# A weight sum by an accumulating transfer, and two more products with hi and lo side by side, in the gate and up stage of a decoder layer

## The chip, the cores and the metric

One core of one Trainium2 chip. The metric is the device time of one execution in microseconds (us). Five engines work side by side: TensorE (PE; its weight loads are listed as PEld), VectorE (DVE), ScalarE (ACT), GpSimd (POOL) and SyncE (SP, which here only issues transfers). Each engine runs its own instructions in the order of its queue and waits on semaphores for the others.

## The reference

One layer of a decoder trunk in float32, with 512 positions and a model width of 1024: a mixer (stick-breaking attention and a gated convolution), a memory cross-attention, a SwiGLU channel sublayer and a final norm. The change touches the first half of the channel sublayer:

```python
hf = rms_norm(x, norm_ffn[l])
gate, up = jnp.split(hf @ w_ffn_in[l], 2, axis=-1)     # w_ffn_in: 1024 x 5632
x = x + (jax.nn.silu(gate) * up) @ w_ffn_out[l]        # w_ffn_out: 2816 x 1024
```

## The kernel before

**Numbers in two parts.** TensorE multiplies in a reduced float32 form (`F32R`). Each operand is split into a hi part (a cast, on ScalarE) and a lo part (the rest, a subtraction on VectorE, `rest_of`, L1006), and a product is the sum of hi x hi, hi x lo and lo x hi.

**Seven products for eight.** The gate and up products of the 2816 hidden columns are made in 22 blocks of 128 columns (`NF = 22`, block number `m`). Each block is a 2 x 2 block product (halves of the contraction; gate and up; halves of the positions), done in Strassen's way (Winograd's form) with seven products, numbered 0 to 6, instead of eight. That needs sums of weights and sums of activations. The activation forms `x2f[k][i]` are made once by `forms_of`, which returns for each of the seven products a hi and a lo part; for those made by `beside`, a third entry is one 512-wide tile with hi and lo next to each other.

**A product.** `product(ps, m, i)` runs over four tiles of the contraction (`KP = 4`). Where hi and lo lie side by side, it is one 512-wide matmul with the hi weights (L909) and one 256-wide one with the lo weights (L917), the four of the latter at the end of the product; the result is then the sum of both halves of the PSUM bank. Otherwise it is three 256-wide matmuls per tile (L914). Products 5 are done side by side in the blocks of `WIDE`.

**Weights of a block.** `ffn_load(m)` fetches two tiles: `wg` (two of the four parts of the weight block) and `ws` (a third part twice, onto which a POOL transfer adds the other two parts, L862). `load_corner` (L868, on SP) fetches the fourth part into a tile `a` of its own. VectorE then makes two more sums: `sum_third` (L874, in place in `wg[:, 0]`) and `sum_last` (L878, `wg[:, 0] + wg[:, 1]` into the second half of the corner tile). The casts are `pair_cast(m, 0)` for products 0 and 1, `pair_cast(m, 1)` for 4 and 2, `pair_cast(m, 2)` for 5 and 6 (the corner tile), `third_cast(m)` for 3 (from `wg[:, 0]`). `ws`, `wg` and the other weight tiles share a few buffers, so a load waits until the old tile in its buffer has been read.

**Results of a block.** Products 0, 3, 4 and 5 add up in one bank `z`, and `reads` copies what each stage needs out of it (ScalarE, L946; L944 in `WIDE` after product 5). Product 1 is in `v`, products 2 and 6 in `y`. `joined_halves` (L936, L937) adds the two halves of a bank to such a copy; `second` is the one for product 2, written to `sb`. `evict` part 0 multiplies by the norm factors (L960), part 1 is the silu (L962), part 2 (L971 in `WIDE`, L974 twice, L978 for even blocks) makes the activations of the second half of the sublayer.

**Order.** The order of TensorE, ScalarE and VectorE is written out by hand. `uses` lists the products: in the steady part 3, 2, 4 of block m, 0, 1 of block m+1, 5, 6 of block m. After each product come its `reads` and then the entries of `todo` under its number, in the order in which `at` put them in; `made` puts a cast at one number and its lo part one number later (two with `late=2`). POOL's and SP's queues are not in this list.

Of the kernel before, what the change touches and what calls it, by code (L numbers as in the profile page):

```python
# [11 lines left out]
ALU = mybir.AluOpType  # L12
# [13 lines left out]
NF = HID // P  # L26
HS = S // 2
# [17 lines left out]
def hybrid_layer(ctx: ExitStack, tc: tile.TileContext, xT_d, memT_d, mem_d, cols_d, wv_d, win_d,  # L45
                 wbr_d, wmix_d, wmq_d, wmk_d, wmv_d, wmo_d, wfi_d, wfo_d, gfin_d, out):
    nc = tc.nc
# [16 lines left out]
    def nm(s):  # L64
        count[0] += 1
        return f"{s}{count[0]}"
# [4 lines left out]
    def tmp(s, cols=512):  # L71
        return tpool.tile([P, cols], F32, tag="t", name=nm(s), padded_shape=[P, 512])

    def f(ap):
        return ap.bitcast(F32)
# [160 lines left out]
    first = nc.scalar.dma_start(gcol, cols_d)  # L236
# [398 lines left out]
    for m in range(KD):  # L635
        sig = []
        for j in range(2):
            if (m, j) not in gates:
                gate(m, j)
            t = gates.pop((m, j))  # L640
# [20 lines left out]
    for m in range(KD):  # L661
# [9 lines left out]
        t = tmp("km", MEM)  # L671
# [27 lines left out]
    def forms_of(xe, xo):  # L699

        b11, b12, b21, b22 = xe[:, :HS], xe[:, HS:], xo[:, :HS], xo[:, HS:]
        c, d = f(unit("c1")), f(unit("c2"))
        n1, t3, n2, t4 = c[:, :HS], c[:, HS:], d[:, :HS], d[:, HS:]
        nc.vector.tensor_tensor(out=n1, in0=b11, in1=b12, op=ALU.subtract)
        nc.vector.tensor_tensor(out=t3, in0=b22, in1=b12, op=ALU.subtract)
        nc.vector.scalar_tensor_tensor(out=n2, in0=n1, scalar=-1.0, in1=b22, op0=ALU.mult,  # L708
                                       op1=ALU.subtract)
        nc.vector.scalar_tensor_tensor(out=t4, in0=n2, scalar=-1.0, in1=b21, op0=ALU.mult,  # L710
                                       op1=ALU.subtract)
        u = unit("xf")
        nc.scalar.copy(u[:, :HS], b11)
        nc.vector.tensor_tensor(out=u[:, HS:], in0=b11, in1=f(u[:, :HS]), op=ALU.subtract)
        a, b = slice(0, HS), slice(HS, S)

        def beside(src, s):
            both = unit(s)
            nc.scalar.copy(both[:, a], src)
            nc.vector.tensor_tensor(out=both[:, b], in0=src, in1=f(both[:, a]), op=ALU.subtract)  # L720
            return both[:, a], both[:, b], both

        first = beside(b21, "xo")
        second, fourth = beside(n1, "xc"), beside(t3, "xc")
        third, fifth = beside(n2, "xd"), beside(t4, "xd")
        last = beside(b22, "xo")
        return [(u[:, a], u[:, b]), first, second, third[:2], fourth[:2], fifth, last]

    def residual(w_dram, act, old, gain, pairs=False):

# [56 lines left out]
    for h in range(MH):  # L787
        q = q_next
        scs = []
        for t2 in range(2):  # L790
            ps = ztile("sc")
            scs.append(ps)
            for i in range(2):
                t = 2 * t2 + i
# [5 lines left out]
        for t2 in range(2):  # L800
# [6 lines left out]
                                           in1=r1s[:, 2 * t2:2 * t2 + 2], op0=ALU.mult,  # L807
# [3 lines left out]
            for i in range(2):  # L811
                t = 2 * t2 + i
# [5 lines left out]
            for i in range(2):  # L818
                nc.vector.tensor_scalar(out=pr[:, i * MEM:(i + 1) * MEM],
                                        in0=pr[:, i * MEM:(i + 1) * MEM],  # L820
# [22 lines left out]

    KP = KD // 2
    raws, corners = {}, {}

    def ffn_load(m):

# [15 lines left out]

    def load_corner(m):

        a22 = corners[m] = fpool.tile([P, 2, 512], F32, tag="w2", name=nm("a22"))
        i = nc.sync.dma_start(a22[:, 0, :], wfi_d[m][:, 3 * 512:])  # L868
        if m < 2:
            after(i, [loads[-6]])  # L870

    def sum_third(m, eng=nc.vector):
        wg, s13 = raws[m]
        eng.tensor_tensor(out=wg[:, 0, :], in0=s13[:, 1, :], in1=wg[:, 0, :], op=ALU.add)  # L874

    def sum_last(m, eng=nc.vector):
        wg = raws[m][0]
        eng.tensor_tensor(out=corners[m][:, 1, :], in0=wg[:, 0, :], in1=wg[:, 1, :], op=ALU.add)  # L878

    wforms = {}  # L880

    def pair_cast(m, which):

        raw = (*raws[m], corners[m])[which]
        hi = wpool.tile([P, 2, 512], F32R, tag="wh", name=nm("wf"))
        lo = wpool.tile([P, 2, 512], F32R, tag="wl", name=nm("wf"))
        nc.scalar.copy(hi, raw)
        for n, i in enumerate(((0, 1), (4, 2), (5, 6))[which]):
            wforms[m, i] = hi[:, n, :], lo[:, n, :]
        return raw, hi, lo  # L890
# [11 lines left out]
    def product(ps, m, i, ks=range(KP)):  # L902

        rests = []
        for k in ks:
            hi, lo = (w[:, k * P:(k + 1) * P] for w in wforms[m, i])
            xh, xl, *both = x2f[k][i]
            if both and (i != 5 or m in WIDE):
                nc.tensor.matmul(ps, hi, both[0], start=i < 3 and k == 0, stop=False,  # L909
                                 skip_group_check=True)  # L910
                rests.append((ps[:, :HS], lo, xh))
                continue
            for j, (a, b) in enumerate(((hi, xh), (hi, xl), (lo, xh))):
                nc.tensor.matmul(ps[:, :HS], a, b, start=i < 3 and k == 0 and j == 0,  # L914
                                 stop=k == KP - 1 and j == 2, skip_group_check=True)
        for operands in rests:
            nc.tensor.matmul(*operands, start=False,  # L917
                             stop=ks[-1] == KP - 1 and operands is rests[-1],
                             skip_group_check=True)

    WIDE = range(5, NF - 3)
    banks, silus = {}, []
    acts = {}

# [10 lines left out]
    def joined_halves(out_, bank, old):  # L935
        nc.vector.tensor_tensor(out=out_, in0=bank[:, :HS], in1=old, op=ALU.add)  # L936
        nc.vector.tensor_tensor(out=out_, in0=bank[:, HS:], in1=out_, op=ALU.add)  # L937

    def reads(m, i):

        b = banks[m]
        z, s, t = b["z"][:, :HS], b["s"], b["t"]
        if i == 5 and m in WIDE:
            nc.scalar.copy(s[:, :HS], b["z"][:, HS:])  # L944
        elif i in (0, 3, 4):
            nc.scalar.copy((s[:, :HS], None, None, s[:, HS:], t[:, :HS])[i], z)  # L946
        elif i == 1:
            joined_halves(b["g"][:, :HS], b["v"], s[:, :HS])
        elif i == 6:
            joined_halves(b["g"][:, HS:], b["y"], s[:, HS:])  # L950

    def second(m):
        b = banks[m]
        joined_halves(b["t"][:, HS:], b["y"], b["t"][:, :HS])

    def evict(m, part):
        b = banks[m]
        g = b["g"]
        if part == 0:
            nc.vector.tensor_tensor(out=g, in0=g, in1=r2b[0], op=ALU.mult)  # L960
        elif part == 1:
            silus.append(nc.scalar.activation(g, g, AF.Silu))  # L962
        else:
            j, odd = divmod(m, 2)
            if not odd:
                acts[j] = f(unit("a1")), f(unit("a2"))
            to = slice(odd * HS, (odd + 1) * HS)
            first = b["z"][:, :HS]
            if m in WIDE:
                first = b["s"][:, :HS]  # L970
                nc.vector.tensor_tensor(out=first, in0=b["z"][:, :HS], in1=first, op=ALU.add)  # L971
            for half, u in enumerate((first, b["t"][:, HS:])):
                sl = slice(half * HS, (half + 1) * HS)
                nc.vector.scalar_tensor_tensor(out=acts[j][half][:, to], in0=u, scalar=-1.0,  # L974
                                               in1=g[:, sl], op0=ALU.mult, op1=ALU.mult)
            if not odd:
                n1 = acts[j][1][:, :HS]
                nc.vector.tensor_tensor(out=n1, in0=acts[j][0][:, :HS], in1=n1, op=ALU.subtract)  # L978
# [5 lines left out]
    m = NF - 1  # L984
# [134 lines left out]
    def at(n, *some):  # L1119
        todo.setdefault(n, []).extend(some)  # L1120

    def made(n, cast, *args, late=1):

        parts = []
        at(n, lambda: parts.append(cast(*args)))
        at(n + late, lambda: rest_of(*parts[0]))
# [14 lines left out]
    for m in range(1, NF - 1):  # L1141
        p = {i: uses.index((m, i)) for i in range(2, 7)}
        q = {i: uses.index((m + 1, i)) for i in range(2)}
        if m > 1:
            at(p[3], lambda m=m: sum_third(m + 1))
            at(p[3], lambda m=m: evict(m - 1, 0))
            at(p[2], lambda m=m: evict(m - 1, 1))
            at(q[0], lambda m=m: evict(m - 1, 2))
            made(p[3], pair_cast, m, 2)
            made(p[2], third_cast, m + 1)  # L1150
        else:
            made(p[4], third_cast, m + 1)
        at(p[4], lambda m=m: second(m))
        if m + 2 < NF:
            at(p[4], lambda m=m: load_corner(m + 2))
        made(q[0], pair_cast, m + 1, 1, late=2)
        at(q[1] if m < NF - 2 else p[4], lambda m=m: sum_last(m + 1))
        if m + 2 < NF:
            made(p[5], pair_cast, m + 2, 0)
    at(uses.index((0, 4)), lambda: second(0))  # L1160
# [33 lines left out]
    with tc.manual_schedule(engines={mybir.EngineType.PE, mybir.EngineType.Activation,  # L1194
# [69 lines left out]
        last = NJ - 2, NJ - 1  # L1264
# [17 lines left out]
        u = [plus("u", res[3][s2], s0[s2]) for s2 in range(2)]  # L1282
# [252 lines left out]
```

## Time and profile before

| | |
|---|---|
| median of 3 runs | 839.92 us (839.05 to 839.99) |
| the profiled execution | 838.75 us, its span 837.0 us |
| busy, share of the span | PE 828.8 us (99%), VectorE 684.6 (82%), ScalarE 463.9 (55%), POOL 161.2 (19%) |
| granted TensorE clock | 0.998 |
| traffic | 143.69 MB, mean 172 GB/s |

The span counts from the first to the last instruction; a row of a timeline gives the start and the duration in us, the engine, the line, the operation with `out<-in`, the shape and, in brackets, how long the engine had been idle before it and what released it. A release time of a wait is inferred from semaphores. Lines L909 to L917 and the others above are those of the code.

### The profile page before, as it was taken

What the parts mean: (1) busy time and instruction counts of PE and PEld (TensorE: products, weight loads), DVE (VectorE), ACT (ScalarE), POOL (GpSimd) and SP (SyncE); (2) the same over time, 40 slices, a digit from 0 to 9 for tenths busy, and PEclk for the clock granted to TensorE, in tenths of its full rate; (3) what the DMA queues carried; (4) which work ended last, traced back from release to release, by engine and by line L of the source; (5) the groups of instructions that cost most, each with busy time, mean ns of one, the idle gap of its engine ahead of it and who ended that gap; (6) DMA issues with size and microseconds to landing.
All of it is one profiled execution on the core that took longest, in us unless ns stands there. A gap on an engine that the chain in (4) does not pass through costs nothing.

```text
span 837.0 us, 11962 instructions
## 1 busy us (share of the span) xinstructions
PE 828.8 (99%) x4374; PEld 714.1 (85%) x4374; DVE 684.6 (82%) x1086; ACT 463.9 (55%) x796; POOL 161.2 (19%) x168
## 2 busy tenths in 40 slices
PE   9999999999999999999999999999999999999996
PEld 7888888888888888888888789999999999888885
DVE  7879899996756576587555698999999999999886
ACT  7567868674332355434444566645555555576654
POOL 0011131110566630173000031111111110000401
PEclk9999999999999999999999999999999999999999
DMA  8552435235687865566431326677767673465552
GB/s 303 155 166 101 122 111 103 74 115 174 228 312 276 304 249 188 182 233 249 148 82 51 101 51 161 167 184 200 197 180 197 176 184 95 170 213 197 180 183 101
DMA packets 51357, 143.69 MB, mean 172 GB/s; under 512 B 5761, under 2 KB 7041, under 8 KB 48482
## 3 DMA queue, kind: packets, MB, share of 16 engines
q1 hardware_dynamic: 41650, 107.89, 38.2%
q0 software_dynamic: 9360, 34.75, 15.8%
q8 instruction: 34, 0.56, 0.3%
q10 hardware_dynamic: 288, 0.28, 0.1%
q14 instruction: 25, 0.20, 0.1%
HBM read 125.20 MB, written 13.64 MB: 166 GB/s over the span
## 4 chain that ended last, share of the span: by engine, by line
PE 99%; DVE 0%; ACT 0%; DVEq 0%; issue 0%
PE z L914 13%; PE p L1228 12%; PE pr L161 8%; PE pr L162 8%; PE pr L163 8%; PE y L909 5%; PE r L162 3%; PE r L163 3%; PE r L161 3%; PE v L288 3%; PE y L917 2%; PE v L909 2%; PE km L666 2%; PE mq L163 2%; PE mq L161 2%; PE mq L162 2%
## 5 line engine op out<-in xcount | busy, mean ns | idle before, releaser
L156 ACT CAST wh<-wr 128x1024 fp32r<-128x1024 f32 x84 | 88.0, 1051 | 144.2 <-issue 80.0
L157 DVE TENSOR_TENSOR wl<-wr,wh 128x1024 fp32r<-128x1024 f32 x84 | 111.0, 1321 | 32.0 <-ACT wh L156 31.9
L161 PE MATMUL pr<-xgh,wh 128*128 128x512 f32 x288 | 112.8, 392 | 0.0
L162 PE MATMUL pr<-xgl,wh 128*128 128x512 f32 x288 | 112.4, 390 | 0.0
L163 PE MATMUL pr<-xgh,wl 128*128 128x512 f32 x288 | 112.3, 390 | 0.0
L611 POOL TENSOR_TENSOR pre<-pre 128x512 f32<-128x512 f32 x44 | 70.9, 1616 | 31.5 <-DMA pre<-in_w_ffn_out_dram 29.2
L862 POOL DMA_DIRECT2D ws<-in_w_ffn_in_dram x22 | 26.6, 1209 | 248.5 <-DVE c L708 54.0
L163 PEld LDWEIGHTS pr<-xgh,wl 128*128 128x128 f32 x288 | 54.1, 188 | 11.5
L161 PEld LDWEIGHTS pr<-xgh,wh 128*128 128x128 f32 x288 | 54.1, 188 | 10.6
L162 PEld LDWEIGHTS pr<-xgl,wh 128*128 128x128 f32 x288 | 54.1, 188 | 10.5
L914 PE MATMUL z<-xd,wf 128*128 128x256 f32 x360 | 47.5, 282 | 0.0
L946 ACT COPY sa<-z 128x256 f32<-128x256 f32 x44 | 16.4, 373 | 51.9 <-PE z L914 51.9
L914 PEld LDWEIGHTS z<-xd,wf 128*128 128x128 f32 x360 | 45.0, 190 | 0.1
L1006 DVE TENSOR_TENSOR wf<-wg,wf 128x1024 fp32r<-128x1024 f32 (+1 forms) x44 | 43.1, 978 | 1.5
L1006 DVE TENSOR_TENSOR wl<-wr,wh 128x1024 fp32r<-128x1024 f32 x33 | 41.0, 1242 | 1.8 <-ACT wh L1073 1.8
L1073 ACT CAST wh<-wr 128x1024 fp32r<-128x1024 f32 x33 | 34.5, 1050 | 5.3 <-ACT f01h L1002 2.6
L914 PE MATMUL z<-xf,wf 128*128 128x256 f32 x264 | 35.4, 283 | 0.0
L914 PE MATMUL z<-xc,wf 128*128 128x256 f32 x264 | 35.1, 283 | 0.0
L914 PEld LDWEIGHTS z<-xf,wf 128*128 128x128 f32 x264 | 33.4, 192 | 0.1
L914 PEld LDWEIGHTS z<-xc,wf 128*128 128x128 f32 x264 | 33.0, 190 | 0.0
L368 DVE TENSOR_TENSOR g<-pr,r0b 128x512 f32<-128x512 f32 x16 | 11.0, 687 | 23.5 <-PE pr L163 23.5
L417 POOL TENSOR_SCALAR_AFFINE_SELECT e<-e 128x128 f32<-128x128 f32 (+1 forms) x24 | 10.7, 447 | 86.6 <-DVE e L470 86.6
(356 smaller groups left out, 2239.9 us busy)
## 6 DMA issues: line engine op xcount, KB each, us to landing
wr<-in_w_in_dram SPq DMA_DIRECT2D x36, 512.0 KB, 3.4
pre<-in_w_ffn_out_dram POOLq DMA_DIRECT2D x11, 1024.0 KB, 8.0
sums<-pre POOLq DMA_DIRECT2D x11, 1024.0 KB, 5.0
ws<-in_w_ffn_in_dram SPq DMA_DIRECT2D x22, 512.0 KB, 4.8
wg<-in_w_ffn_in_dram SPq DMA_DIRECT2D x22, 512.0 KB, 4.7
ws<-in_w_ffn_in_dram POOLq DMA_DIRECT2D x22, 512.0 KB, 5.7
wr<-sums SPq DMA_DIRECT2D x22, 512.0 KB, 4.0
wr<-in_w_ffn_out_dram SPq DMA_DIRECT2D x16, 512.0 KB, 3.7
```

The costliest lines, as they stand in the source:

```text
L156: after(nc.scalar.copy(h2, raw), lead[-1:])
L157: lows.append(nc.vector.tensor_tensor(out=l2, in0=raw, in1=f(h2), op=ALU.subtract))
L161: nc.tensor.matmul(ps, a[0], b[0], start=start, stop=False, **kw)
L162: nc.tensor.matmul(ps, a[0], b[1], start=False, stop=False, **kw)
L163: nc.tensor.matmul(ps, a[1], b[0], start=False, stop=stop, **kw)
L611: nc.gpsimd.tensor_tensor(out=t[:, a, :], in0=t[:, a, :], in1=t[:, b, :], op=ALU.add)
L862: nc.gpsimd.dma_start(s13, a[:, 0:4:3, :], accum_op=ALU.add)
L909: nc.tensor.matmul(ps, hi, both[0], start=i < 3 and k == 0, stop=False, skip_group_check=True)
L914: nc.tensor.matmul(ps[:, :HS], a, b, start=i < 3 and k == 0 and j == 0, stop=k == KP - 1 and j == 2, skip_group_check=True)
L1006: nc.vector.tensor_tensor(out=lo, in0=src, in1=f(hi), op=ALU.subtract)
L1073: nc.scalar.copy(hi, raw)
L1228: nc.tensor.matmul(res[i][s2], a[:, ts], b, start=j == 0 and n == 0, stop=n == 2 and j == (BEHIND - 1 if (i, s2) == (5, 1) else NJ - 1))
```

## The change

For blocks 3 to 20 (`OWN`) the corner has no tile of its own any more. The sum of `sum_last` is made by an accumulating transfer on POOL, which adds `wg[:, 0]` onto `wg[:, 1]` in place, right after `sum_third`. After that, and after `third_cast` has been read out, `load_corner` fetches the fourth part into `wg[:, 0]`, so that `wg` itself becomes the corner tile. The load's place in the list is product 5 of the iteration before; `pair_cast(m, 2)` stands at product 4 instead of product 3, and its lo part at product 0 of the next block instead of product 2.

`WIDE` grows from blocks 5 to 18 to blocks 3 to 19, and in it product 4 is side by side too, since `forms_of` now hands out the joint tile for it. Then `reads` copies the whole bank `z` after product 4 (512 columns instead of 256), and `second` becomes `folded`: one 512-wide addition of the bank of product 2 to that copy, and one that adds the two halves. The copy after product 5 goes to `sb` instead of `sa`.

```diff
         second, fourth = beside(n1, "xc"), beside(t3, "xc")
         third, fifth = beside(n2, "xd"), beside(t4, "xd")
         last = beside(b22, "xo")
-        return [(u[:, a], u[:, b]), first, second, third[:2], fourth[:2], fifth, last]
+        return [(u[:, a], u[:, b]), first, second, third[:2], fourth, fifth, last]
 
     def residual(w_dram, act, old, gain, pairs=False):
 
 
     KP = KD // 2
     raws, corners = {}, {}
+    OWN = range(3, NF - 1)
 
     def ffn_load(m):
 
 
     def load_corner(m):
 
+        if m in OWN:
+            nc.sync.dma_start(raws[m][0][:, 0, :], wfi_d[m][:, 3 * 512:])
+            return
         a22 = corners[m] = fpool.tile([P, 2, 512], F32, tag="w2", name=nm("a22"))
         i = nc.sync.dma_start(a22[:, 0, :], wfi_d[m][:, 3 * 512:])
         if m < 2:
 
     def sum_last(m, eng=nc.vector):
         wg = raws[m][0]
+        if m in OWN:
+            nc.gpsimd.dma_start(wg[:, 1, :], wg[:, 0, :], accum_op=ALU.add)
+            return
         eng.tensor_tensor(out=corners[m][:, 1, :], in0=wg[:, 0, :], in1=wg[:, 1, :], op=ALU.add)
 
     wforms = {}
 
     def pair_cast(m, which):
 
-        raw = (*raws[m], corners[m])[which]
+        raw = (*raws[m], raws[m][0] if m in OWN else corners[m])[which]
         hi = wpool.tile([P, 2, 512], F32R, tag="wh", name=nm("wf"))
         lo = wpool.tile([P, 2, 512], F32R, tag="wl", name=nm("wf"))
         nc.scalar.copy(hi, raw)
         for k in ks:
             hi, lo = (w[:, k * P:(k + 1) * P] for w in wforms[m, i])
             xh, xl, *both = x2f[k][i]
-            if both and (i != 5 or m in WIDE):
+            if both and (i not in (4, 5) or m in WIDE):
                 nc.tensor.matmul(ps, hi, both[0], start=i < 3 and k == 0, stop=False,
                                  skip_group_check=True)
                 rests.append((ps[:, :HS], lo, xh))
                              stop=ks[-1] == KP - 1 and operands is rests[-1],
                              skip_group_check=True)
 
-    WIDE = range(5, NF - 3)
+    WIDE = range(3, NF - 2)
     banks, silus = {}, []
     acts = {}
 
 
         b = banks[m]
         z, s, t = b["z"][:, :HS], b["s"], b["t"]
-        if i == 5 and m in WIDE:
-            nc.scalar.copy(s[:, :HS], b["z"][:, HS:])
+        if m in WIDE and i == 4:
+            nc.scalar.copy(t, b["z"])
+        elif m in WIDE and i == 5:
+            nc.scalar.copy(t[:, :HS], b["z"][:, HS:])
         elif i in (0, 3, 4):
             nc.scalar.copy((s[:, :HS], None, None, s[:, HS:], t[:, :HS])[i], z)
         elif i == 1:
         elif i == 6:
             joined_halves(b["g"][:, HS:], b["y"], s[:, HS:])
 
+    def folded(out_, bank, old):
+        nc.vector.tensor_tensor(out=old, in0=bank, in1=old, op=ALU.add)
+        nc.vector.tensor_tensor(out=out_, in0=old[:, :HS], in1=old[:, HS:], op=ALU.add)
+
     def second(m):
         b = banks[m]
+        if m in WIDE:
+            folded(b["t"][:, HS:], b["y"], b["t"])
+            return
         joined_halves(b["t"][:, HS:], b["y"], b["t"][:, :HS])
 
     def evict(m, part):
             to = slice(odd * HS, (odd + 1) * HS)
             first = b["z"][:, :HS]
             if m in WIDE:
-                first = b["s"][:, :HS]
+                first = b["t"][:, :HS]
                 nc.vector.tensor_tensor(out=first, in0=b["z"][:, :HS], in1=first, op=ALU.add)
             for half, u in enumerate((first, b["t"][:, HS:])):
                 sl = slice(half * HS, (half + 1) * HS)
         q = {i: uses.index((m + 1, i)) for i in range(2)}
         if m > 1:
             at(p[3], lambda m=m: sum_third(m + 1))
+            if m + 1 in OWN:
+                at(p[3], lambda m=m: sum_last(m + 1))
+                at(p[5], lambda m=m: load_corner(m + 1))
             at(p[3], lambda m=m: evict(m - 1, 0))
             at(p[2], lambda m=m: evict(m - 1, 1))
             at(q[0], lambda m=m: evict(m - 1, 2))
-            made(p[3], pair_cast, m, 2)
+            made(p[4] if m in OWN else p[3], pair_cast, m, 2)
             made(p[2], third_cast, m + 1)
         else:
             made(p[4], third_cast, m + 1)
         at(p[4], lambda m=m: second(m))
-        if m + 2 < NF:
+        if m + 2 < NF and m + 2 not in OWN:
             at(p[4], lambda m=m: load_corner(m + 2))
         made(q[0], pair_cast, m + 1, 1, late=2)
-        at(q[1] if m < NF - 2 else p[4], lambda m=m: sum_last(m + 1))
+        if m + 1 not in OWN:
+            at(q[1] if m < NF - 2 else p[4], lambda m=m: sum_last(m + 1))
         if m + 2 < NF:
             made(p[5], pair_cast, m + 2, 0)
     at(uses.index((0, 4)), lambda: second(0))
```

## The prediction

> **What bounds the kernel now.** I read the chain of waits first, then the windows of the gate and up stage by block, then the timelines of three engines over one block. TensorE is the chain:
>
> ```profile
> PE 99%; DVE 0%; ACT 0%; DVEq 0%; issue 0%
> ```
>
> Nothing waits for TensorE to be fed. The windows below are one block each (the columns are the stretch, its length, busy time of PE, PEld, DVE, ACT and POOL, the granted clock, DMA share, GB/s):
>
> ```profile
> 551.32:561.26 9.94, 9.94 (x74) 9.42 (x73) 9.54 (x18) 5.00 (x8) 1.20 (x1) 1.00 0.74 189
> 581.09:591.00 9.91, 9.91 (x69) 9.20 (x69) 9.66 (x17) 5.38 (x9) 1.06 (x2) 1.00 0.68 184
> ```
>
> The first is a block whose fifth product is in twelve matmuls, the second one whose fifth product is already side by side. The granted clock is 1.00. VectorE is busy for 9.66 of 9.91 us: it keeps up, with little to spare, so its order of work decides whether TensorE stays fed. I call "product i of block m" what the code calls (m, i). TensorE's order is 3, 2, 4 of block m, 0, 1 of block m+1, 5, 6 of block m. This is iteration m = 7 on TensorE, from product 3 (575.22) to product 6 (583.73); columns are start, duration:
>
> ```profile
> 575.22 1.59 PE L914 MATMUL z<-xd,wf 128*128 128x256 f32 x12
> ...
> 578.05 1.59 PE L914 MATMUL z<-xc,wf 128*128 128x256 f32 x12
> 579.49 1.60 PE L914 MATMUL z<-xf,wf 128*128 128x256 f32 x12
> 580.92 1.09 PE L909 MATMUL v<-xo,wf 128*128 128x512 f32 x4
> ...
> 582.33 1.09 PE L909 MATMUL z<-xd,wf 128*128 128x512 f32 x4
> 583.25 0.64 PE L917 MATMUL z<-xd,wf 128*128 128x256 f32 x4
> 583.73 1.09 PE L909 MATMUL y<-xo,wf 128*128 128x512 f32 x4
> ```
>
> VectorE in the same time:
>
> ```profile
> 575.42 0.42 DVE L936 TENSOR_TENSOR fg<-y,sa 128x256 f32<-128x256 f32 x1
> ...
> 577.47 0.69 DVE L874 TENSOR_TENSOR wg<-ws,wg 128x512 f32<-128x512 f32 x1
> 578.08 0.68 DVE L960 TENSOR_TENSOR fg<-fg,r0b 128x512 f32<-128x512 f32 x1
> 578.68 1.22 DVE L1006 TENSOR_TENSOR wf<-a,wf 128x1024 fp32r<-128x1024 f32 x1
> 579.97 0.69 DVE L1006 TENSOR_TENSOR wf<-wg,wf 128x512 fp32r<-128x512 f32 x1
> 580.58 0.42 DVE L936 TENSOR_TENSOR sb<-y,sb 128x256 f32<-128x256 f32 x1
> 581.03 0.42 DVE L937 TENSOR_TENSOR sb<-y,sb 128x256 f32<-128x256 f32 x1
> 581.37 0.41 DVE L971 TENSOR_TENSOR sa<-z,sa 128x256 f32<-128x256 f32 x1
> 581.82 0.42 DVE L974 SCALAR_TENSOR_TENSOR a<-sa,fg 128x256 f32<-128x256 f32 x1
> 582.16 0.42 DVE L974 SCALAR_TENSOR_TENSOR a<-sb,fg 128x256 f32<-128x256 f32 x1
> 582.62 0.42 DVE L978 TENSOR_TENSOR a<-a,a 128x256 f32<-128x256 f32 x1
> 582.96 0.41 DVE L936 TENSOR_TENSOR fg<-v,sa 128x256 f32<-128x256 f32 x1
> ...
> 583.75 0.68 DVE L878 TENSOR_TENSOR a<-wg 128x512 f32<-128x512 f32 x1
> 584.35 1.22 DVE L1006 TENSOR_TENSOR wf<-ws,wf 128x1024 fp32r<-128x1024 f32 x1
> ```
>
> The row at 578.68 is what matters: the lo half of the corner pair, the weights of products 5 and 6. It ends at 579.90, over 3 us before product 5 reads it (L917, 583.25). It also sits in a gap: the next instruction, at 579.97, has to wait for ScalarE's cast of the third weight, which waits in turn for L960:
>
> ```profile
> 576.85 0.37 ACT L946 COPY sa<-z 128x256 f32<-128x256 f32 x1 [1.46 <-PE z L914]
> 577.12 1.06 ACT L887 CAST wf<-a 128x1024 fp32r<-128x1024 f32 x1
> 578.79 0.63 ACT L962 ACTIVATE fg<-fg 128x512 f32<-128x512 f32 x1 [0.62 <-DVE fg L960]
> 579.33 0.61 ACT L895 CAST wf<-wg 128x512 fp32r<-128x512 f32 x1
> 579.84 0.36 ACT L946 COPY sb<-z 128x256 f32<-128x256 f32 x1
> ```
>
> That cast ends at 579.94, and L1006 starts at 579.97.
>
> **The change, part by part.** *Fewer matmuls.* A product in twelve takes 579.49 - 578.05 = 1.44 us, one side by side 583.73 - 582.33 = 1.40; the two windows differ by 0.03 us for one product, which I take. Product 4 changes in 17 blocks (3 to 19) and product 5 in three more (3, 4, 19): 20 x 0.03 = 0.6 us less, on the path.
>
> *The weight sum leaves VectorE.* L878 goes in 18 blocks (3 to 20), 584.35 - 583.75 = 0.60 us each. VectorE does not end last, so this gives nothing by itself.
>
> *The second combination on whole banks.* L936 and L937 at 580.58 occupied 581.37 - 580.58 = 0.79 us. Now there is one 128x512 add, 0.69 us (as L874; all 512-wide adds here lie near) and some 0.03 to the instruction that needs it, then a 256-wide one, after which the next starts 0.34 later: 1.06 us, so 0.27 more in 17 blocks. ScalarE's copy before it goes from 0.36 us to 0.58, from this row (median of a 512-wide copy out of PSUM):
>
> ```profile
> L1273 ACT COPY s<-p x2: 578/584/589, 773.7 to 774.2; 128x512 f32<-128x512 f32 x2
> ```
>
> It starts at 579.84 and ends at 580.42, before VectorE gets there at 580.58, so it costs nothing; were VectorE there earlier, it would be the limit.
>
> *The corner pair is cast later.* This is the step that costs. In blocks 3 to 20 the cast goes from behind product 3 to behind product 4, and its lo half from VectorE's place at 578.68 to the list of the next product, behind the entries already there: the four of `evict(m - 1, 2)` (L971, L974 twice, L978). The place given up is worth nothing: 579.97 stays, since the cast of the third weight sets it. VectorE idles about 1.2 us there, then has everything else ahead of the lo half. For block 7: 580.58 + 1.06 = 581.64 (L971); L971 to L978 and what follows took 582.96 - 581.37 = 1.59, so the lo half starts at 583.23 and ends at 584.45. ScalarE's hi half runs from 580.4 to 581.5 and is in time for product 5 at 582.33. The wide form reads lo only in its fifth matmul, L917, 583.25 less 0.03 for the shorter product 4 = 583.22. How fast TensorE follows VectorE shows in one place of the trace:
>
> ```profile
> 463.61 0.69 DVE L181 TENSOR_TENSOR oml<-om,omh 128x512 fp32r<-128x512 f32 x1 [1.54 <-ACT omh L179]
> ...
> 464.36 0.19 PEld L162 LDWEIGHTS r<-oml,wh 128*128 128x128 f32 x1 [0.24 <-DVE oml L181]
> ```
>
> The weight load follows 0.06 us after the end (464.30), and I add 0.11 for the matmul that has nothing to overlap it with: 0.17 in all, an estimate. Stall: 584.45 + 0.17 - 583.22 = 1.40 us. Where m is even, L978 is absent: 0.46 less, 0.94. In block 3 L971 is absent (block 2 is not side by side): 0.95. Block 20 keeps the narrow product 5, which needs lo at its third matmul, 0.24 after 582.33, and keeps the last weight sum in front (0.60); with no L978 and the old 0.79 the lo half ends at 584.32, so the stall is 1.92.
>
> Sum: 8 odd blocks (5 to 19) x 1.40 + 8 even ones (4 to 18) x 0.94 + 0.95 + 1.92 = 21.6; less 0.6 gives +21.0 us. It does not heal itself: the next iteration hangs on the end of product 6, which moves with the stall. VectorE behind the late lo half has L936/L937 (0.79) and L1006 (1.22) to do, until 586.5; product 6 also ends at about 586.5 (584.62 + 0.48 for L917 + 1.40), and the next L936 starts 0.20 after that, as at 575.42: it starts each block on time, and loses the same again.
>
> *The transfers.* The accumulating transfer waits for L874 (end 578.16). The one it resembles, L862 on POOL with 512 KB, lands so long after its issue (us):
>
> ```profile
> DMA to landing us min/median/max: 5.4/5.7/8.3
> ```
>
> The corner load, L868 on SP with 256 KB, moves behind it, since it overwrites what the sum read; it lands after
>
> ```profile
> DMA to landing us min/median/max: 2.4/3.0/6.4
> ```
>
> Together that is 8.7 us at the medians, 14.7 at the maxima. The cast needs the corner one period later, at 580.42 + 11.1 = 591.5, that is 13.3 us after 578.16, and may be 1.4 late before it delays the lo half. Behind the waiting instructions stand, on POOL, the accumulate of L862 for three blocks ahead and, on SP, the loads of `ws` and `wg`. `wg` now comes free only with the late lo half (584.45) instead of with L878:
>
> ```profile
> wg<-in_w_ffn_in_dram SPq DMA_DIRECT2D x22, 512.0 KB, 4.7
> ```
>
> It is there 5 us later, and the first cast of it comes about a period after that. So I take zero for the transfers. The bounds are zero and, where the corner load also queues on SP behind that load of `wg` and both take long, about 1 us per block. By the Trainium skill, "DMA: Bandwidth & Descriptors", section "Anatomy of one DMA", a POOL transfer takes about 2.0 us plus its bytes at 436 GB/s, 2.6 us here as an estimate; the sum would be the same 21.0, and this case's own accumulates (5.4 at least) are slower than that. On POOL it is 18 more issues of about 1.2 us (the one in the first window's POOL column), on an engine busy for some 1 us of ten.
>
> Ends of the unknown: VectorE at 580.28 instead of 580.58 (ScalarE's copy 0.20 behind product 4's end, as at 576.85 behind product 3's) takes 17 x 0.3 = 5 us off, and no restart cost 2 more: +14. The transfers add up to 18: +39. I take +21, from the rows of the block itself.
>
> **The rivals.**
>
> *The cover holds.* If the lo half comes out ahead of `evict(m - 1, 2)` on VectorE, it starts at 581.64 and ends at 582.86, before 583.05, when it is wanted: no stall, 0.6 us gained, 839.3. Point of decision: the lo half ends 0.94 us (even) or 1.40 (odd) earlier than worked out. For it: ScalarE and VectorE have less in sum than before. Against: VectorE's rows above run in exactly the written order. 11 in 100.
>
> *The transfers come late too.* If accumulate and corner load together exceed some 14.8 us, the cast waits and the pair is later still: at 1 us a block in 18 blocks, 861 + 18 = 879. For it: DMA share is already 0.68 to 0.74, and these tiles are held a period longer. Against: the medians. 7 in 100.
>
> *The clock.* If gaps of about 1 us made the throttle halve the clock for the rest of each block, 9.9 us a block would come on top: 861 + 17 x 9.9 = 1029. The windows show 1.00 but have no gaps. The Trainium skill, "TensorE: Matmul & The Clock Gate", section "Why this matters for your kernels", puts the limit at gaps of about 3 us; by that rule nothing happens here, and no row here shows a gap of that length. 2 in 100.
>
> **How the numbers follow.** The profiled execution took 838.75 us (span 837.0); the median is 839.92. 838.75 + 21.0 = 859.8, against the median 860.9; I say 861. My forecast has 80 in 100. Its bounds give 854 (+14) at the low end, and part of the transfers' cost (0.5 us a block) 870 at the high end; I open the low end to 852 for rounding in the stalls. Outside lie the cover case, the clock and most of the late transfers. What a measurement can tell from no change is 0.2%, 1.7 us: slower 0.89 (80 + 7 + 2); the cover case's 0.6 us is "same", 0.09, with 0.02 left for faster.
>
> **What would show it.** Right: L917 weight loads of z wait on L1006, once a block, about 1.4 and 0.9 us in turn; blocks of about 11.3 and 10.8 us; VectorE idle about 1.2 us before the 512-wide L1006, waiting for L895; the lo half of the corner right behind L974 or L978. Rival transfers: ScalarE's cast of the corner waits on a DMA. Cover: blocks of 9.88 us. I would be wrong if the list order on VectorE were not as read, or if product 5 needed lo later than its fifth matmul.

## The result and the profile after

The changed kernel takes 860.24 us (median of 5 runs, 860.0 to 860.63) against 839.64 (5 runs): 1.0247 times as long, 95% interval 1.0232 to 1.0262. The profiled execution's span is 858.3 us against 837.0, 21.3 more. The prediction said 861, +21.0.

The chain of waits on the page of after is no longer TensorE alone:

```profile
PE 78%; DVE 16%; ACT 3%; issue 2%; DVEq 0%
```

The waits of the gate and up stage (engine, line, what it waited for: us in total, times, longest). L924 was L917 before, L1022 was L1006, L902 was L895, L894 was L887:

```profile
PEld z L924 <- DVE wf L1022: 22.3, 17, 1.5
DVE wf L1022 <- ACT wf L902: 21.8, 18, 1.2
...
ACT wf L894 <- DMA wg<-in_w_ffn_in_dram: 0.2, 1, 0.2
```

In 17 blocks the lo weights of product 5 are late; in block 20, whose product 5 is narrow, they are late too, by L921. In 18 blocks VectorE idles 1.2 us for the cast of the third weight. ScalarE waited for a transfer once, for 0.2 us. Two blocks, an odd and an even one, as windows (columns as in the prediction):

```profile
564.23:575.49 11.26, 10.15 (x66) 8.93 (x64) 9.54 (x17) 5.49 (x10) 2.11 (x2) 1.00 0.84 201
575.49:586.29 10.80, 10.15 (x65) 8.92 (x64) 9.12 (x16) 5.49 (x10) 2.11 (x2) 1.00 0.80 196
```

They alternate so through the stage, but for the first (11.08 us) and the last. VectorE is busy for less of it than before (9.12 to 9.54 of some 11 us, 9.66 of 9.91 then): it has less to do, but it waits, and the lo half comes late in its order. Block 7 on TensorE, the block of the prediction's rows:

```profile
586.76 1.09 PE L916 MATMUL z<-xd,wf 128*128 128x512 f32 x4
588.96 0.74 PE L924 MATMUL z<-xd,wf 128*128 128x256 f32 x4 [1.11 <-DVE wf L1022]
589.54 1.09 PE L916 MATMUL y<-xo,wf 128*128 128x512 f32 x4
```

Product 5 takes 589.54 - 586.76 = 2.78 us, 1.38 more than 1.40. VectorE in the same block:

```profile
582.54 0.69 DVE L976 TENSOR_TENSOR fg<-fg,r0b 128x512 f32<-128x512 f32 x1
584.43 0.69 DVE L1022 TENSOR_TENSOR wf<-wg,wf 128x512 fp32r<-128x512 f32 x1 [1.21 <-ACT wf L902]
585.04 0.68 DVE L962 TENSOR_TENSOR sb<-y,sb 128x512 f32<-128x512 f32 x1
585.76 0.43 DVE L963 TENSOR_TENSOR sb<-sb 128x256 f32<-128x256 f32 x1
586.10 0.42 DVE L987 TENSOR_TENSOR sb<-z,sb 128x256 f32<-128x256 f32 x1
586.55 0.76 DVE L990 SCALAR_TENSOR_TENSOR a<-sb,fg 128x256 f32<-128x256 f32 x2
587.35 0.42 DVE L994 TENSOR_TENSOR a<-a,a 128x256 f32<-128x256 f32 x1
587.69 1.22 DVE L1022 TENSOR_TENSOR wf<-wg,wf 128x1024 fp32r<-128x1024 f32 x1
588.83 0.42 DVE L943 TENSOR_TENSOR fg<-v,sa 128x256 f32<-128x256 f32 x1
```

The row at 587.69 is the lo half of the corner pair. Before, it stood directly behind the multiplication by the norm factors (L976, there L960) and filled the gap that is now the 1.21 us in brackets. Now it stands behind L962 to L994 and ends at 588.91; the weight load of L924 follows at 588.96.

### The profile page after: what moved, and what is told of

It reads as the page before. It is cut to its first block, busy times and chain, and to the rows that moved or that the text cites. A ratio compares the mean times of both kernels' runs of the same rounds, so it can differ in the third digit from the quotient of the medians.

```text
span 858.3 us, 11822 instructions
## 1 busy us (share of the span) xinstructions
PE 833.4 (97%) x4294; PEld 708.8 (83%) x4294; DVE 682.9 (80%) x1071; ACT 467.3 (54%) x799; POOL 174.3 (20%) x186
## 4 chain that ended last, share of the span: by engine, by line
PE 78%; DVE 16%; ACT 3%; issue 2%; DVEq 0%
PE p L1248 12%; PE pr L161 8%; PE pr L162 8%; PE pr L163 8%; DVE wf L1022 7%; PE r L162 3%; PE r L161 3%; PE r L163 3%; PE v L288 3%; PE y L916 2%; PE km L666 2%; PE mq L163 2%; PE mq L161 2%; PE mq L162 2%; PE br L163 2%
## 5 line engine op out<-in xcount | busy, mean ns | idle before, releaser
L1022 DVE TENSOR_TENSOR wf<-wg,wf 128x1024 fp32r<-128x1024 f32 (+1 forms) x62 | 65.0, 1048 | 21.9 <-ACT wf L902 21.8
L863 POOL DMA_DIRECT2D ws<-in_w_ffn_in_dram x22 | 26.7, 1213 | 139.0 <-DVE c L707 52.9
L921 PE MATMUL z<-xd,wf 128*128 128x256 f32 x324 | 43.1, 283 | 1.6 <-DVE wf L1022 1.6
L894 ACT CAST wf<-wg 128x1024 fp32r<-128x1024 f32 x40 | 42.1, 1052 | 2.0 <-PE r L162 1.8
L1022 DVE TENSOR_TENSOR wl<-wr,wh 128x1024 fp32r<-128x1024 f32 x33 | 40.2, 1219 | 3.0 <-ACT wh L1089 2.8
L921 PEld LDWEIGHTS z<-xd,wf 128*128 128x128 f32 x324 | 40.6, 191 | 1.9 <-DVE wf L1022 1.9
L883 POOL DMA_DIRECT2D wg<-wg x18 | 16.6, 925 | 120.4 <-DVE wg L878 82.8
L921 PE MATMUL z<-xf,wf 128*128 128x256 f32 x264 | 35.4, 283 | 0.0
L921 PEld LDWEIGHTS z<-xf,wf 128*128 128x128 f32 x264 | 33.4, 192 | 0.1
L978 ACT ACTIVATE fg<-fg 128x512 f32<-128x512 f32 x22 | 13.9, 632 | 35.6 <-DVE fg L976 35.6
L953 ACT COPY sb<-z 128x256 f32<-128x256 f32 x17 | 6.3, 373 | 41.2 <-PE z L924 23.4
```

The costliest lines, as they stand in the source:

```text
L863: nc.gpsimd.dma_start(s13, a[:, 0:4:3, :], accum_op=ALU.add)
L1022: nc.vector.tensor_tensor(out=lo, in0=src, in1=f(hi), op=ALU.subtract)
```

## The experiments

Four runs pull the change's parts apart, four more isolate the late cast and seek a place where the sum costs nothing, and two settle what those left open. They stand here by topic. Each is compared with the kernel before on the same chip.

**The lo half ahead of evict part 2.** (`e1_lo_first`)

```diff
+            made(p[4] if m in OWN else p[3], pair_cast, m, 2)
             at(q[0], lambda m=m: evict(m - 1, 2))
-            made(p[4] if m in OWN else p[3], pair_cast, m, 2)
```

> The changed kernel with one move: on VectorE the lo half of the corner pair comes ahead of the entries of evict part 2 (m - 1) instead of behind them; hi cast, weight sum and products 4 and 5 stay. Theory A (the lo half is late only because of what stands ahead of it): it ends at 582.86 in the frame of block 7 of the prediction, in time, so the stall goes and the time is 839 to 840 us. Theory B (VectorE's cycle: L943/L944 0.80, lo of products 0 and 1 1.25, L878 0.61, L976 to the third weight's lo 1.89 because ScalarE's silu and cast lie between, that lo 0.61, L962/L963 1.06, corner lo 1.14, evict part 2 1.36 on average, L943/L944 0.79, lo of 4 and 2 1.14: 10.65 us a block, whatever the order, as long as the 1.2 us gap in front of the third weight's lo is empty; TensorE needs only 9.88): 17 x (10.65 - 9.88) and some 0.8 for block 20, less 0.6, is +13; 852 to 854 us, with the stalls now anywhere in the block.

852.86 us (852.53 to 852.98), ratio 1.0162 (1.0145 to 1.0179): theory B. The blocks, from product 1 to product 1:

```profile
583.45 1.09 PE L916 MATMUL v<-xo,wf 128*128 128x512 f32 x4
593.86 1.09 PE L916 MATMUL v<-xo,wf 128*128 128x512 f32 x4
604.71 1.09 PE L916 MATMUL v<-xo,wf 128*128 128x512 f32 x4
```

The two blocks take 10.41 and 10.85 us, 10.63 on average against the 10.65 of VectorE's cycle. The instructions in the cycle are shorter in sum than a block of TensorE; it is the gap that makes it longer:

```profile
594.11 0.69 DVE L1022 TENSOR_TENSOR wf<-wg,wf 128x512 fp32r<-128x512 f32 x1 [1.21 <-ACT wf L902]
```

VectorE multiplies (L976), ScalarE makes the silu and then casts the third weight, VectorE takes that cast: a round trip which VectorE used to fill with the lo half. With the order repaired but the gap still empty, two thirds of the loss stay.

**The cast back at its place.** (`e2_cast_back`)

```diff
-            made(p[4] if m in OWN else p[3], pair_cast, m, 2)
+            made(p[3], pair_cast, m, 2)
```

> The changed kernel with the cast of the corner pair back behind product 3 and its lo half back at product 2, where it fills VectorE's gap; weight sum by transfer, corner load into wg and products 4 and 5 side by side stay. Theory (the late cast alone made it slower): the stall at L924 goes; VectorE's cycle is 9.5 us. 839.5 us if sum and corner load land in time. They have 8.8 us from the end of L878 to the cast, 1.4 more before it hurts; in the changed kernel they took about 8.6 (3.7 and 4.1 us at the medians, with the waits between), so in some blocks the cast may wait for a transfer: up to 846. Rival (the transfers or the wider products cost the time themselves): still 855 to 861.

851.91 us (847.32 to 853.18), ratio 1.014 (1.0111 to 1.0169): a miss. The stall of product 5 at L924 is gone and many blocks take 9.88 to 9.89 us, but others take up to 11.8, and the times scatter (the profile is of the run of 847.32):

```profile
ACT wf L894 <- DMA wg<-in_w_ffn_in_dram: 41.4, 16, 4.2
```

I had the landing of the corner load too short. It took 2.8 to 7.3 us, 5.9 at the median, where 4.1 had been seen. It now follows 0.7 to 2.4 us behind the load of a `wg` tile on SP, where it went ahead of that load before; I take this to be the reason, but no run isolates it. So neither the theory's number nor the rival as put (products or transfers cost that much in the changed kernel) holds: the old place of the cast asks more of the transfers than the changed kernel did.

**The transfer and the late cast without the wider products.** (`e3_own_only`: `product`, `reads`, `second`, `evict`, `forms_of` and `WIDE` as before)

> The kernel before with the weight sum by transfer, the corner load into wg and the late cast in blocks 3 to 20 alone; product 4 stays in twelve matmuls, product 5 side by side in blocks 5 to 18 as before. Theory (order of VectorE's work): second is 0.27 us shorter, so the lo half ends 0.27 earlier and is wanted where it was: stalls of 1.10 (odd) and 0.64 (even) in the side by side blocks, 0.9 to 1.8 in blocks 3, 4, 19 and 20, whose narrow product 5 wants lo at its third matmul; sum 17, so 856 to 857 us. Rival (the wider products make it slow): about 840.

862.96 us (862.34 to 863.91), ratio 1.0283 (1.0267 to 1.0298). The stalls in the regular part are those expected: blocks of 10.99 and 10.54 us, that is 9.91 + 1.08 and + 0.63. Two blocks took 13.59 and 14.21 us, some 6.3 us more than their neighbours; without them it would be 856.7. In these ScalarE waits for the corner:

```profile
580.28 1.04 ACT L894 CAST wf<-wg 128x1024 fp32r<-128x1024 f32 x1 [3.67 <-DMA wg<-in_w_ffn_in_dram]
```

and on POOL the sum (L883) stood behind the accumulate of `ws` (L863), before which POOL had been idle for 12.02 us:

```profile
570.34 1.20 POOL L863 DMA_DIRECT2D ws<-in_w_ffn_in_dram  x1 [12.02 <-DVE wf L1017]
571.05 1.43 POOL L883 DMA_DIRECT2D wg<-wg  x1
```

The profile puts that wait down to VectorE. The accumulate also waits for the plain load of the same `ws` tile, issued on SP at 564.52, and I take that load to be what came last; it is inferred, not shown. Part of the 6.3 us is the clock: behind the two waits of TensorE in these blocks (1.54 and 2.44 us) the granted clock was 0.50 for some 3 us.

**The wider products alone.** (`e4_wide_only`)

```diff
-    OWN = range(3, NF - 1)
+    OWN = range(0)
```

> The kernel before with products 4 and 5 side by side in blocks 3 to 19 alone; the weight sum stays on VectorE and the corner in a tile of its own, cast behind product 3. Theory: 0.6 us less on TensorE, but VectorE's cycle grows from 9.84 to 10.11 us where TensorE needs 9.88; that lag of 0.23 us a block reaches 3.9 us over 17 blocks, of which some 2.2 us of lead on the other lo halves swallow most: about 1.7 us of stall in the last blocks, 840 to 841.5 us. Rival (VectorE keeps up): 839.1. If it is slower than 845, the wider products, not the late cast, made the change slow.

842.6 us (842.28 to 842.72), ratio 1.0039 (1.0024 to 1.0054). The mechanism holds: six blocks take 9.87 to 9.89 us, the ones behind them 10.08 to 10.16, VectorE's cycle with the sum still on it. The lead I gave it was too long (six blocks, not nine), hence 1.1 us past the range. VectorE (the third busy time of the row) in one of the later blocks, busy for 9.86 of 10.10 us:

```profile
644.00:654.10 10.10, 10.10 (x64) 8.81 (x64) 9.86 (x17) 5.27 (x10) 1.32 (x2) 1.00 0.66 174
```

So the wider products cost 3 us by themselves, as 0.27 us a block more on VectorE outweighs 0.03 less on TensorE; they need the sum off VectorE.

**The late cast alone.** (`e7_late_alone`, from the kernel before)

```diff
-            made(p[3], pair_cast, m, 2)
+            made(p[4] if m > 2 else p[3], pair_cast, m, 2)
...
-            at(p[4], lambda m=m: load_corner(m + 2))
+            at(p[5] if m > 2 else p[4], lambda m=m: load_corner(m + 2))
```

> The kernel before with the pair cast alone moved behind product 4 in blocks 3 to 20 (its lo half to product 0 of the next block), the corner's next load behind it; sum on VectorE, no accumulating transfer, products as before. Theory: VectorE's cycle is 0.80 + 1.25 + 0.61 + 1.89 + 0.61 + 0.79 + 1.36 + 1.14 + 0.79 + 0.60 + 1.14 = 10.98 us a block, more than the 11.01 and 10.54 (10.78) that the lo half's lateness gives: 17 x 1.07 + 1.5 for block 20 = +20, 857 to 860. Rival (the late cast costs only together with the transfers or the wider products): 839 to 845.

860.74 us (859.73 to 861.64), ratio 1.0254 (1.0239 to 1.0269), with no accumulating sum and no wider product in it. Blocks of 10.74 and 11.19 us, 10.97 on average against 10.98. The first took 13.65. In it TensorE stood still for 1.91 us and was then granted half its clock (the third number from the end of the second row) for some 3 us:

```profile
545.74 2.40 PE L914 MATMUL z<-xd,wf 128*128 128x256 f32 x10 [1.91 <-DVE wf L1006]
546.20:549.20 3.00, 3.00 (x13) 2.73 (x12) 2.01 (x3) 0.00 (x0) 0.00 (x0) 0.50 0.65 200
```

The matmuls behind that wait, up to the lo matmuls of product 6, took 2.19 + 1.56 us, against 1.30 + 0.93 for the same ones a block later: 1.5 us, more than the 0.7 us by which the time lies past the range. The late cast, with the later corner load that goes with it, is enough to lose all that the changed kernel loses. Its limit here is VectorE's cycle, which still has the sum on it; in the changed kernel it is the lateness of the lo half (11.03 us a block).

**A tile of its own for the corner.** (`e5_own_tile`; the cast is back behind product 3 and the load of the fourth part at its old place)

```diff
         i = nc.sync.dma_start(a22[:, 0, :], wfi_d[m][:, 3 * 512:])
+        if m in OWN:
+            nc.sync.dma_start(a22[:, 1, :], wfi_d[m][:, 512:2 * 512])
...
-            nc.gpsimd.dma_start(wg[:, 1, :], wg[:, 0, :], accum_op=ALU.add)
+            nc.gpsimd.dma_start(corners[m][:, 1, :], wg[:, 0, :], accum_op=ALU.add)
```

> The changed kernel with the corner back in a tile of its own: two loads (the fourth part and the second part of the weight block) as early as before the change, the third weight added onto the second half by the accumulating transfer, cast behind product 3 and lo half at product 2 as before the change; products 4 and 5 side by side in 3 to 19. Theory (a cycle of VectorE of 9.5 us, with the gap in front of the third weight's lo filled, and a sum that now lands some 4 us before it is wanted): no stall, 0.6 us less than before: 838.6. Rival (accumulating transfers disturb the other transfers or VectorE): above 840, with casts waiting on DMA.

850.98 us (849.04 to 853.28), ratio 1.0139 (1.0118 to 1.016): the rival's number, but not every block. Mostly two take 9.88 to 9.89, and the third 10.84 to 13.75. POOL shows why; L882 is the sum:

```profile
576.31 1.21 POOL L863 DMA_DIRECT2D ws<-in_w_ffn_in_dram  x1 [8.68 <-DVE sb L961]
577.05 1.41 POOL L882 DMA_DIRECT2D a<-wg  x1
...
582.62 0.86 POOL L882 DMA_DIRECT2D a<-wg  x1 [4.16 <-DVE wg L877]
```

The third weight for the sum at 577.05 had been there since 572.8 (L877 at 572.10). In every third block the sum stands behind an accumulate that is late itself, and the cast waits for the sum:

```profile
584.07 1.05 ACT L893 CAST wf<-a 128x1024 fp32r<-128x1024 f32 x1 [3.38 <-DMA a<-wg]
```

The bracket at 576.31 names VectorE; the load of `ws` that the accumulate adds to was issued on SP at 570.84, and such loads land 5.4 us later at the median, at 576.2. So the load is the likely reason that the accumulate was late, by inference; the next run tests only the order.

**That order put right.** (`e9_own_tile_ordered`; `after` adds an order and no wait)

```diff
-        nc.gpsimd.dma_start(s13, a[:, 0:4:3, :], accum_op=ALU.add)
+        i = nc.gpsimd.dma_start(s13, a[:, 0:4:3, :], accum_op=ALU.add)
+        if m - 2 in sum_dma:
+            after(i, [sum_dma[m - 2]])
```

> The own tile with one thing added: on POOL the accumulate of ws for block m + 3 comes behind the accumulating sum for block m + 1, every block. With the own tile, in every third block the sum stood on POOL behind such an accumulate, which was waiting for its load (issued at 577.05 instead of some 572.9, and the cast waited 3.4 us for it). Theory: with that gone nothing is late, VectorE's cycle is 9.5 us, TensorE's 9.88: 838.4 to 839.0, 0.6 us under the kernel before. Rival (transfers as such are too slow): above 842, with casts still waiting on DMA.

839.27 us (median of 11 runs; ten from 838.62 to 839.52, one of 843.08 that no trace explains) against 839.59 (15 runs), ratio 1.0 (0.9991 to 1.0009). In the profiled run sixteen blocks in a row take 9.88 to 9.89 us, and the chain of waits is TensorE's again:

```profile
PE 99%; DVE 0%; ACT 0%; DVEq 0%; issue 0%
```

So two ideas of the change (the sum off VectorE, products 4 and 5 side by side in 17 blocks) work together without a stall once the lo half is in its gap and the sum is not held up on POOL's queue; the third, the corner in `wg` itself, is given up here. The 0.6 us that the blocks show (9.88 instead of 9.91) is too little for the whole kernel's time to tell. The price is traffic, in a stretch of 40 us:

```profile
600.00:640.00 40.00, 40.00 (x263) 36.47 (x262) 37.75 (x63) 22.85 (x38) 8.26 (x9) 1.00 0.97 248
```

a DMA share of 0.97 (the prediction's rows have 0.68 and 0.74), as the second part of the weight block is read twice.

**The late cast with that tile.** (`e6_own_tile_late`, and with the order put right `e10_late_ordered`: cast behind product 4, its lo half behind evict part 2)

> The same early loads into a tile of its own, but the pair cast behind product 4 and its lo half behind evict part 2, as in the changed kernel. Theory (in the changed kernel the transfers cost nothing, the late lo half all): 860, with blocks of 11.26 and 10.8 us. Rival (the changed kernel's transfers had a part in it): below 858.

879.46 us (876.02 to 881.55), ratio 1.0486 (1.0467 to 1.0504): outside both. Six blocks were late (12.64, 14.55, 12.00, 11.50, 15.64 and 16.38 us, where the changed kernel has 10.8 or 11.3); ScalarE stood idle for up to 5.8 us ahead of its casts of the corner, and the profile names no releaser for it.

> The late own tile with the same order on POOL: the pair cast behind product 4 and its lo half behind evict part 2, but the sum and its loads apart from the changed kernel's tile. Theory (the late lo half alone gives the changed kernel's time): 860, blocks of 11.26 and 10.8 us. Rival (with transfers on time the late lo half costs less): below 856.

Three runs took 872.71 to 875.27 us, ratio 1.0406 (1.039 to 1.0422); a fourth took 1683.8, which nothing here explains, and is not in the ratio. Again above both. Up to block 11 it runs as the changed kernel does:

```profile
542.33 1.09 PE L918 MATMUL v<-xo,wf 128*128 128x512 f32 x4
...
641.55 1.09 PE L918 MATMUL v<-xo,wf 128*128 128x512 f32 x4
```

nine blocks in 99.22 us, where the changed kernel's nine sum up to 99.35; then casts wait 2.7 to 5.4 us, and blocks of 14.26, 12.19, 17.21 and, as the last, 14.74 follow. The profile names the sum for the longest of these waits; the two before it end 3.4 us after the sum's issue, which is its landing at the median. Why the sum is issued late is not shown; a tile that is released late is also loaded late, and two loads hang on it. Behind the waits of 2.60 and 4.47 us on TensorE the granted clock was 0.50 again. The pair shows that the late lo half costs the same wherever the corner lies, as long as transfers are on time; it does not give a whole run free of late transfers.

**The sum as an addition on POOL.** (`e8_pool_add`)

```diff
-                at(p[3], lambda m=m: sum_last(m + 1))
-                at(p[5], lambda m=m: load_corner(m + 1))
+                at(p[3], lambda m=m: sum_last(m + 1, nc.gpsimd))
```

(with `OWN` empty and the cast at its old place)

> The changed kernel with the sum as an ordinary addition on POOL into the corner's own tile (1.62 us each by the one such row of the trace before), cast and lo half in their old places. Theory 1 (POOL and VectorE work side by side): as the own tile, 838.6 to 839.5. Theory 2 (an addition on POOL holds up VectorE: in the trace before, one lo half of 128x512 took 1.78 instead of 0.69 us beside such an addition): some 1.1 to 1.6 us a block on VectorE, a cycle of 10.6 to 11.1 against 9.88, 852 to 861.

852.49 us (851.3 to 853.17), ratio 1.0154 (1.0139 to 1.017): theory 2, at the low end of its range. The addition on POOL, and VectorE's instruction beside it, which takes 0.69 us by itself:

```profile
574.38 1.78 POOL L886 TENSOR_TENSOR a<-wg 128x512 f32<-128x512 f32 x1
```

```profile
574.11 2.61 DVE L1023 TENSOR_TENSOR wf<-wg,wf 128x512 fp32r<-128x512 f32 x1
```

VectorE's ends at 576.72, 0.56 us after POOL's at 576.16. Over the stage the lo half of the corner takes 2.08 us on average instead of 1.22. The Trainium skill, "SBUF — State Buffer", section "SBUF: two separate sides", says that VectorE and GpSimd share one pair of ports, that an instruction of either holds it to its end, and that VectorE instructions with two SBUF inputs take part against a GpSimd instruction that reads SBUF. This trace agrees as far as VectorE's instruction, which has two SBUF inputs, lasted until POOL's was over; that its row begins 0.27 us before POOL's, and that it was held all the same, is not explained by the rows.

## Why the prediction was right

*The lo half moved behind evict part 2.* Forecast stalls 1.40 (odd blocks), 0.94 (even), 0.95 (block 3), 1.92 (block 20). Measured from product 5 to the product behind it: 1.38, 0.92, 1.20 and 1.90. Block 3 was mis-sized by 0.25. The prediction has VectorE waiting for product 6 at the start of each block, as block 8 does (second row). In block 3 it did not wait; it came straight from the lo half of `ws`, 0.32 us after product 6's end at 535.89, where block 8 needs 0.04 (591.10 to 591.14):

```profile
536.21 0.42 DVE L943 TENSOR_TENSOR fg<-y,sa 128x256 f32<-128x256 f32 x1
591.14 0.42 DVE L943 TENSOR_TENSOR fg<-y,sa 128x256 f32<-128x256 f32 x1 [0.31 <-PE y L924]
```

The sum of the stalls is 1.20 + 8 x 1.38 + 8 x 0.92 + 1.90 = 21.5, forecast 21.6. Less the 0.6 saved that is 20.9; of the 21.3 by which the profiled span grew, another 0.2 lie ahead of the stage (503.67 against 503.45 at its first product 1).

*The gap of 1.2 us that remains.* 1.21 us, 18 times, as worked out.

*How fast TensorE follows.* I put 0.17 us. The lo half ends at 588.91, product 6 begins 0.63 later instead of 0.47 or 0.48: 0.15 or 0.16.

*The second combination and the copy.* 1.06 us from L962 to L987 (586.10 - 585.04), as forecast; the copy of 512 columns costs nothing.

*Transfers.* Zero was right for this kernel. The sum and the corner load landed after

```profile
DMA to landing us min/median/max: 3.3/3.7/6.2
```

```profile
DMA to landing us min/median/max: 2.5/4.1/6.4
```

against 5.4 to 8.3 and 2.4 to 6.4 assumed: the sum was put too long and the corner load, at the median, too short; together they take 7.8 us at the medians, forecast 8.7. There was room: the corner loads issued at 577.14 and 587.15 are cast at 584.78 and 596.05, 7.6 and 8.9 us later. By the Trainium skill, "DMA: Bandwidth & Descriptors", section "Anatomy of one DMA", cited in the prediction, the sum's transfer would take 2.6 us, an estimate; the measurement decides, and it is longer. The zero belongs to this kernel's order alone. With the cast back ScalarE waited 16 times for the corner, and without the wider products three times, up to 3.67 us, in blocks nearly as long as here: in both the rival "the transfers come late too" came true.

*The clock.* Granted 1.00 in blocks with gaps of 1.1 us (the windows above), and in block 20 behind its gap of 1.65 us; so the rival did not come true. It was closer than I thought. The late cast alone shows 0.50 behind a gap of 1.91 us, and the transfer without the wider products shows it behind gaps of 1.54 and 2.44 us; gaps of 2.16 us (the late cast with an own tile) and 2.31 us (the own tile) left it at 1.00. What decides between them is not shown. The Trainium skill, "TensorE: Matmul & The Clock Gate", section "Why this matters for your kernels", cited in the prediction, puts the limit at gaps of about 3 us; these runs had the clock halved by shorter ones, and the measurement decides.

*The rival "the cover holds" was priced wrongly.* I gave it 839.3, from the one place where the lo half is wanted. The first experiment made just that case, and it took 852.86: I had not added up VectorE's cycle with the empty gap, 10.65 us a block. Its point of decision was not the order behind the gap but the gap. The forecast is not touched by this, since 11.0 us from TensorE's side is longer than 10.65.

*VectorE's sum leaving "gives nothing by itself".* No run tests this part by itself. The wider products alone show that they cost 3 us with the sum still on VectorE. In the changed kernel it was worth something too: with the sum, VectorE's cycle would be 10.65 + 0.60 = 11.25 us, an estimate from the cycle above and the 0.60 us that the prediction gives the sum, and a block took 11.03. The prediction looked at what ends last in a block and not at VectorE's whole round. Its total is not touched, since it was worked out with the sum already off VectorE.

## What to carry to other kernels

Before moving an instruction on a busy engine, ask what its old place hid: here it stood in the gap of a round trip through another engine, and moving it left the gap empty and put all its length in front of a matmul. Add up the round of each engine, its waits for others included, and set the sum against the bound engine's period; busy time alone said that VectorE had got less to do, and it had. When work goes to a transfer queue, look at what that queue's neighbours wait for: an accumulate which waits for its load holds back the sum behind it.

## What the runs showed of the hardware that I had not expected

With the DMA engines busy for 0.97 of a stretch, as with the ordered own tile, all transfers still arrived in time for TensorE to run without a stall; what had made the own tile's sum late was its place in POOL's queue, the one thing that differs between the two runs. There the accumulating sum landed after 3.8 to 6.2 us, against 3.3 to 6.2 in the changed kernel. An accumulating transfer issued by POOL left VectorE's instructions as they were (the 128x1024 lo halves at 1.22 us on average in that kernel), while an ordinary addition on POOL drew one of them out from 0.69 to 2.61 us. Gaps on TensorE as short as 1.54 us could be followed by half the granted clock for some 3 us, while gaps of 1.1 us in every other block left it at 1.00.
